# A hybrid decoder layer on one core: cached attention of the decoded rows, two rows on shared partitions

## The chip, the core and the metric

The kernel runs on one core of a Trainium2 chip. The core has a matrix engine (TensorE, PE in the profile), a vector engine (VectorE, DVE), a scalar engine (ScalarE, ACT), a general engine (GpSimd, POOL) and a queue engine (SyncE, SP) that here only issues transfers. Each works through its own list of instructions in order, and semaphores make one wait for another. On-chip memory has 128 partitions; matmuls write to PSUM banks. The metric is the device time of one launch in microseconds: 1455.61 us as the median of 3 runs (1454.94 to 1456.85). About 0.2% of it, 2.9 us, is what these runs can tell from no change.

## The reference

One layer of a decoder is applied to a prompt of 256 tokens and to 8 decoded rows (one new token of each of 8 sequences), with d = 2048 in float32. The two share all weights, so the kernel carries them as N = 264 columns of one matrix. The part that matters here is the attention to memory, 4 heads of width 512 and 256 memory tokens:

```
xq = (rmsnorm(x, g_xa) @ w_xa_q).reshape(B, L, XA_HEADS, XA_DH)
s = jnp.einsum('blhd,bmhd->bhlm', xq, mk.astype(dt)).astype(jnp.float32) * (XA_DH ** -0.5)
p = jax.nn.softmax(s, axis=-1).astype(dt)
o = jnp.einsum('bhlm,bmhd->blhd', p, mv.astype(dt)).reshape(B, L, D_MODEL)
x = x + o @ w_xa_o
```

For the prompt, keys and values mk, mv are computed from a memory of 256 tokens by w_xa_k and w_xa_v. For the decoded rows they come from a cache: every row b and head h has its own 256 x 512 keys and values. So each decoded row is a query vector against matrices of its own, 512 KB of K and 512 KB of V for each of 32 pairs of row and head. Before this part lie a recurrent mixer and its output projection, behind it a feed-forward block with three times 2048 x 5632 weights, and a last norm.

## The kernel before

Everything is held transposed: channels on the partitions in blocks of 128, tokens along the free dimension. A projection goes through a list of steps, `steps`. A step of 2048 x 128 weights loads two halves of 128 x 1024 (SP's queue, tile `raw`, three steps ahead), splits each into a high and a low part in float32r (tile `w`: ACT copies the high part, DVE subtracts to get the low one) and multiplies: 48 matmuls of 264 columns for 16 blocks of channels, three each (high x high, high x low, low x high). `w` has four buffers, each of half a step, so a split waits until PE has read the half-step four earlier, and a step's split is emitted one step ahead of its matmuls with high priority.

The order of the work: the steps run in program order, and beside them stand generators ("side work") that the function `pump` advances after every step, until the planned clocks of DVE and ACT reach that of PE plus 0.5 us. A `yield STEP` ends a generator's turn in that step. The framework's scheduler then orders each engine's list from priorities and dependencies; only SP's list, and PE's in a few places, is kept as written.

The steps around the change are: 16 blocks of `w_q` (the query projection; `evac_q` takes each block's 256 prompt columns into a tile and its 8 decoded columns into `qsm`), then for each head four steps of `w_k` and four of `w_v` for the prompt's memory, then 16 steps of `w_o`. Two generators do the decoded rows' attention beside them, from the fourth block of `w_q` on:

- `dec_k` (line 1167) goes over heads and rows. For each it loads `kc` (128 channels x 4 blocks x 256 tokens) and `vc` from POOL's queue into buffers of the pool `B` (26 buffers), multiplies the four channel blocks of K by the query's per-partition scalars and adds them up in `acc` (first product on ACT, three multiply-adds on DVE), and splits `acc` into `ds` (high on ACT, low on POOL, line 1187).
- `dec_v` (line 1191) sums `ds` over the partitions with two matmuls against `onesr`, a 128 x 128 matrix of ones, which leaves the scores on all partitions (tile `ax`). It takes the maximum (DVE), the exponential and its sum (ACT), and multiplies the four blocks of V by the probabilities with an accumulated sum (DVE), into `osm`. At a head's end `osm` is divided by the sum of the exponentials and `st["dh"]` tells `attend(h)` that the head is done.

`attend(h)` is the prompt's attention; its last part copies and splits `osm` into the columns 256 to 263 of the operands of `w_o` (tiles `oh` and `ol`, groups `B<-osm`). The first `w_o` steps multiply the blocks of heads 0 to 2 first, and those of head 3 when they are there (`pe_o`, line 1361).

The loops and lists are in these functions:

Of the kernel before, what the change touches and what calls it, by code (L numbers as in the profile page):

```python
# [22 lines left out]
N = T + NS  # L23
RGB = 8
H = 4
# [16 lines left out]
STEP = object()  # L42
# [52 lines left out]
def layer_kernel(ctx: ExitStack, tc, xT, memT, vec, wrg, w_in, w_out, w_q, w_k, w_v, w_o,  # L95
# [39 lines left out]
    class Arr:  # L135


        def __init__(self, nb, w=N, dt=F32):
            self.t, self.nb, self.w, self.dt = {}, nb, w, dt
# [7 lines left out]
        def __call__(self, c):  # L147
            return self.tile(c // 4)[:, c % 4, :]
# [119 lines left out]
    def unturn(ps):  # L268

        return ps.rearrange("p (a b) -> p b a", b=2)  # L270
# [9 lines left out]
    st = {}  # L280
# [63 lines left out]
    onesr = const.tile([P, P], F32R, name="onesr")  # L344
# [799 lines left out]
    qsm = const.tile([P, KC, NS], F32, name="qsm")  # L1144
    osm = const.tile([P, KC, NS], F32, name="osm")
    ssm = const.tile([P, H, NS], F32, name="ssm")

    def evac_q(j):
        def f(ps):
            if j == 0:  # L1150
                qn["t"] = Arr(KC, T)
            p2, m = unturn(ps[:, :N]), N // 2
            dve.tensor_mul(qn["t"](j)[:, :m], p2[:, 0, :], rstd[:, :m])
            dve.tensor_mul(qn["t"](j)[:, m:T], p2[:, 1, : T - m], rstd[:, m:T])
            dve.tensor_mul(qsm[:, j, :], p2[:, 1, T - m:], rstd[:, T:N])
            qn["n"] = j + 1
            if j == 3:
                with tc.issue_after(st["split"].ins):
                    act.activation(onesr, ones, AF.Copy)
                st["dk"] = side(dec_k(), 5)  # L1160
                st["dv"] = side(dec_v(), 4)
        return f

    pairs = []
    infl = {"n": 0}

    def dec_k():
        for h in range(H):
            while qn["n"] < 4 * h + 4:
                yield STEP  # L1170
            for b in range(NS):
                while infl["n"] >= NFL:
                    yield STEP
                infl["n"] += 1
                kc = B([P, 4, T])
                pool_e.dma_start(kc, kcT[h, b])  # L1176
                w = sb.tile([P, 264], F32, tag="dw", bufs=2, name=nm("dw"))
                ws = sb.tile([P, 2, T], F32R, tag="ds", bufs=2, name=nm("ds"))
                vc = B([P, 4, T])
                pool_e.dma_start(vc, vcT[h, b])  # L1180
                acc = w[:, 0:T]
                q = [qsm[:, 4 * h + c, b: b + 1] for c in range(4)]
                act.activation(acc, kc[:, 0, :], AF.Copy, scale=q[0])
                for c in range(1, 4):
                    dve.scalar_tensor_tensor(acc, kc[:, c, :], q[c], acc, op0=OP.mult, op1=OP.add)
                act.activation(ws[:, 0], acc, AF.Copy)
                pool_e.tensor_sub(ws[:, 1], acc, ws[:, 0].bitcast(F32))  # L1187
                pairs.append((h, b, w, vc, ws))
                yield 1.1

    def dec_v():
        done, cur = 0, None
        while done < H * NS:
            nxt = None
            if pairs:
                nxt = pairs.pop(0)
                ps = bank("ax")
                pe.matmul(by2(ps[:, :T]), onesr, turn(nxt[4][:, 0]), start=True, stop=False)
                pe.matmul(by2(ps[:, :T]), onesr, turn(nxt[4][:, 1]), start=False, stop=True)
# [5 lines left out]
            h, b, w, vc, _, ps = todo  # L1205
            mx, p = w[:, T: T + 1], w[:, :T]
            dve.tensor_reduce(mx, ps[:, :T], axis=AX.X, op=OP.max)
            dve.tensor_scalar(mx, mx, -XSCALE, None, op0=OP.mult)
            act.activation(halves(p), unturn(ps[:, :T]), AF.Exp, scale=XSCALE, bias=mx,
                           accum_out=ssm[:, h, b: b + 1])  # L1210
            yield 0.5
            for c in range(4):
                dve.scalar_tensor_tensor(vc[:, c, :], vc[:, c, :], 1.0, p, op0=OP.mult, op1=OP.mult,
                                         accum_out=osm[:, 4 * h + c, b: b + 1])
            infl["n"] -= 1
            done += 1
            if done % NS == 0:
# [244 lines left out]
    for i, (src, cols, pef, evf, need) in enumerate(steps):  # L1462
# [26 lines left out]
        ps = pef(i)  # L1489
# [147 lines left out]
```

## Time and profile before

| What | Number |
|---|---|
| median of 3 runs | 1455.61 us |
| the profiled execution | 1455.66 us |
| its span, first to last instruction | 1453.9 us |
| PE busy | 1439.6 us, 99% |
| DVE busy | 1046.8 us, 72% |
| ACT busy | 794.4 us, 55% |
| POOL busy | 129.7 us, 9% |
| read from HBM, written | 314.36 MB, 12.86 MB |

The span begins with the first instruction and leaves out 1.8 us of the execution's own time. Busy time of PE counts overlapping matmuls once, and the mean of one matmul (for example 279 ns) is its time from issue to end, of which the next one overlaps a part; how fast PE really goes is seen from the distance between starts. In the profile's groups, `out<-in` names tiles, and most lines are L60, a helper that records the operations. "Idle before" is time in which the engine stood still just before that group, with the engine that ended it.

### The profile page before, as it was taken

How to read it: one execution, taken by the hardware profiler on the slowest of the kernel's cores; microseconds unless marked ns; L12 is line 12 of the kernel's file. 1: busy time of each engine (PE TensorE's matmuls, PEld its weight loads, DVE VectorE, ACT ScalarE, POOL GpSimd, SP SyncE). 2: the span in 40 equal slices, each digit the busy share in tenths (PEclk: the TensorE clock that was granted, in tenths of full speed). 3: DMA queues.
4: the chain of work that ended last, by engine and by line, in shares of the span. 5: the costliest groups of instructions: out<-in, count | busy, mean ns of one | idle time of the engine just before them, and what ended most of it. 6: DMA issues, size and time to landing. Idle time of an engine off the chain costs nothing.

```text
span 1453.9 us, 30117 instructions
## 1 busy us (share of the span) xinstructions
PE 1439.6 (99%) x12059; PEld 1413.9 (97%) x12059; DVE 1046.8 (72%) x1999; ACT 794.4 (55%) x1279; POOL 129.7 (9%) x206
## 2 busy tenths in 40 slices
PE   9999999999999999999999999999999999999997
PEld 8998999999999999999999999999999999999997
DVE  7966897898899999977676565555656655556564
ACT  7678685665556666656554444334444434444463
POOL 0001210000124343410000000000000000000000
PEclk9999999999999999999999999999999999999999
DMA  9755996558789977955666565655555565656573
GB/s 284 236 174 170 305 378 235 174 169 282 268 328 358 340 288 286 364 175 196 195 192 199 191 200 191 197 195 195 197 196 196 191 201 190 199 192 197 166 239 126
DMA packets 100766, 329.18 MB, mean 226 GB/s; under 512 B 11057, under 2 KB 19937, under 8 KB 100625
## 3 DMA queue, kind: packets, MB, share of 16 engines
q1 hardware_dynamic: 84336, 271.95, 56.2%
q0 software_dynamic: 15424, 54.22, 10.3%
q8 instruction: 94, 1.54, 0.4%
q10 hardware_dynamic: 864, 1.09, 0.2%
q14 instruction: 48, 0.39, 0.1%
HBM read 314.36 MB, written 12.86 MB: 225 GB/s over the span
## 4 chain that ended last, share of the span: by engine, by line
PE 56%; DVE 1%; issue 1%; POOL 0%; ACT 0%; DVEq 0%; DMA 0%; POOLq 0%; ACTq 0%
PE mm L60 55%; PE ax L60 1%; DVE B L60 1%; DVE dw L60 0%; POOL ds L1187 0%; DVE w L60 0%; POOL B L1241 0%; ACT B L60 0%; DVE c L60 0%; POOL o_v L1285 0%; ACT dw L60 0%; DVE t L60 0%; ACT ds L60 0%; DMA o_k<-t 0%; DVEq L1614 0%
## 5 line engine op out<-in xcount | busy, mean ns | idle before, releaser
L60 PE MATMUL mm<-B,w 128*128 128x264 f32 (+1 forms) x10960 | 1281.7, 279 | 2.7 <-DVE w L60 2.3
L60 PEld LDWEIGHTS mm<-B,w 128*128 128x128 f32 x10960 | 1260.8, 189 | 11.1 <-DVE w L60 2.8
L60 DVE TENSOR_TENSOR w<-raw,w 128x1024 fp32r<-128x1024 f32 (+1 forms) x522 | 625.3, 1200 | 307.7 <-ACT w L60 307.1
L60 ACT ACTIVATE w<-raw 128x1024 fp32r<-128x1024 f32 (+1 forms) x522 | 536.3, 1029 | 524.0 <-PE mm L60 358.4
L60 PE MATMUL mm<-w,B 128*128 128x512 f32 x384 | 86.9, 380 | 0.1
L60 PEld LDWEIGHTS mm<-w,B 128*128 128x128 f32 x384 | 70.6, 189 | 9.8 <-DVE w L60 0.5
L1526 POOL TENSOR_TENSOR B<-B,rstd 128x264 f32<-128x264 f32 x4 | 2.8, 740 | 802.9 <-ACT rstd L60 802.9
L60 DVE TENSOR_TENSOR t<-mm,rstd 128x264 f32<-128x264 f32 x96 | 41.5, 433 | 28.9 <-PE mm L60 28.8
L60 DVE SCALAR_TENSOR_TENSOR B<-B,dw 128x256 f32<-128x256 f32 x128 | 53.4, 471 | 3.2 <-ACT dw L60 3.0
L60 DVE TENSOR_TENSOR xres<-xres,mm 128x264 f32<-128x264 f32 (+1 forms) x81 | 34.3, 425 | 29.2 <-PE mm L60 29.2
L60 DVE SCALAR_TENSOR_TENSOR dw<-B,qsm,dw 128x256 f32<-128x256 f32 x96 | 49.1, 516 | 2.5 <-ACT dw L60 1.7
L1187 POOL TENSOR_TENSOR ds<-dw,ds 128x256 fp32r<-128x256 f32 x32 | 36.2, 1131 | 106.5 <-ACT ds L60 106.4
L60 PE MATMUL ax<-B,B 128*128 128x256 f32 (+3 forms) x280 | 44.3, 300 | 0.0
L60 PEld LDWEIGHTS ax<-B,B 128*128 128x128 f32 x280 | 38.8, 191 | 1.9
L60 ACT ACTIVATE B<-xres,vecs 128x264 fp32r<-128x264 f32 (+1 forms) x64 | 32.3, 504 | 3.1 <-DVE xres L60 1.6
L60 ACT ACTIVATE t<-xres 128x264 f32<-128x264 f32 (+1 forms) x53 | 21.1, 410 | 16.2 <-DVE xres L60 16.2
L60 ACT ACTIVATE dw<-B,qsm 128x256 f32<-128x256 f32 x32 | 16.3, 509 | 23.7 <-issue 10.0
L1176 POOL DMA_DIRECT2D B<-kcT x32 | 17.4, 544 | 116.4 <-DVE B L60 103.3
L60 DVE SCALAR_TENSOR_TENSOR B<-xres,vecs,B 128x264 fp32r<-128x264 f32 x48 | 23.4, 489 | 4.0 <-ACT B L60 4.0
L60 ACT ACTIVATE dw<-B,B 128x128 f32<-128x128 f32 x64 | 20.8, 393 | 9.0 <-DMA B<-scr 6.4
L60 ACT ACTIVATE B<-t 128x264 fp32r<-128x264 f32 (+1 forms) x60 | 24.2, 410 | 2.1 <-DVE t L60 2.1
L60 ACT ACTIVATE dw<-ax,dw 128x256 f32<-128x256 f32 x32 | 15.0, 470 | 18.8 <-DVE dw L60 16.7
(173 smaller groups left out, 696.7 us busy)
## 6 DMA issues: line engine op xcount, KB each, us to landing
raw<-w_gu SPq DMA_DIRECT2D x176, 512.0 KB, 4.3
raw<-w_d SPq DMA_DIRECT2D x80, 512.0 KB, 3.6
raw<-w_in SPq DMA_DIRECT2D x74, 512.0 KB, 5.4
raw<-w_out SPq DMA_DIRECT2D x32, 512.0 KB, 4.2
B<-kcT POOLq DMA_DIRECT2D x32, 512.0 KB, 8.7
raw<-w_q SPq DMA_DIRECT2D x32, 512.0 KB, 5.6
B<-vcT POOLq DMA_DIRECT2D x32, 512.0 KB, 10.0
raw<-w_k SPq DMA_DIRECT2D x32, 512.0 KB, 4.9
```

Of the source, the lines that this page charges most:

```text
L60: return f(*a, **k)
L1176: pool_e.dma_start(kc, kcT[h, b])
L1187: pool_e.tensor_sub(ws[:, 1], acc, ws[:, 0].bitcast(F32))
L1526: e.tensor_mul(st["y"](c), st["y"](c), r)
```

## The change

Two decoded rows are put on the 128 partitions together, row 2b on partitions 0 to 63 and row 2b+1 on 64 to 127. A partition then holds 8 blocks of 256 tokens of one row's K (two neighbouring channels' four blocks) where it held 4. So there are 16 pairs instead of 32 rows, and each pair has eight products on K (one on ACT, seven on DVE) and eight on V. `onesr` becomes block-diagonal, ones in the two 64 x 64 corners, so that one pair of matmuls gives both rows' scores, each on its own half of the partitions. Maximum, scaling, exponential, split and subtraction are done once for a pair.

K and V no longer take a new buffer for each row. Each has a `Ring` of two buffers of half a pair, loaded with 128 partitions of 4 KB (`load`, called again when a half has been read). The queries have to be moved to the new partitions (`swap_q`: a POOL copy and four POOL transfers of 64 partitions x 64 bytes for each head) and the outputs back (`swap_o`). The sum over partitions of a pair is taken one step later than before, by one more `yield STEP` ahead of `pairs.append`.

```diff
+            if j % 4 == 3:
+                swap_q(j // 4)
             if j == 3:
                 with tc.issue_after(st["split"].ins):
-                    act.activation(onesr, ones, AF.Copy)
+                    act.activation(onesr, ones, AF.Copy, scale=0.0)
+                    for part in (LOW, HIGH):
+                        act.activation(onesr[part, part], ones[part, part], AF.Copy)
...
+    NB2 = NS // 2
+    q2 = const.tile([P, H, 2, 4, NB2], F32, name="q2")
+    q3 = const.tile([P, 2, 2, 4, NB2], F32, name="q3")
+    o2, o3 = q2, q3
+    LOW, HIGH = slice(0, 64), slice(64, P)
+    by_row = lambda x: x.rearrange("p c (b s) -> p s c b", s=2)
+    def swap_q(h):
+        pool_e.tensor_copy(q3[:, h % 2], by_row(qsm[:, 4 * h: 4 * h + 4, :]))
+        for q, part in enumerate((LOW, HIGH)):
+            for e in range(2):
+                pool_e.dma_start(q2[part, h, e], q3[e: P: 2, h % 2, q])
+    def swap_o(h):
+        rec = ssm[:, h, 0: NB2]
+        dve.reciprocal(rec, rec)
+        o = o2[:, h].rearrange("p g c b -> p (g c) b")
+        dve.tensor_mul(o, o, rec.rearrange("p (c b) -> p c b", c=1).to_broadcast([P, 8, NB2]))
+        for q, part in enumerate((LOW, HIGH)):
+            for e in range(2):
+                pool_e.dma_start(o3[e: P: 2, h % 2, q], o2[part, h, e])
+        pool_e.tensor_copy(by_row(osm[:, 4 * h: 4 * h + 4, :]), o3[:, h % 2])
+    class Ring:
+        def __init__(self, src):
+            self.t, self.at = [B([P, 4, T]), B([P, 4, T])], 0
+            self.src = src.rearrange("h b p c t -> h (b p) c t")
+            self.load()
+            self.load()
+        def load(self):
+            u = self.at
+            if u < H * NB2 * 2:
+                self.at = u + 1
+                b = u // 2 % NB2 * 2 * P + u % 2
+                pool_e.dma_start(self.t[u % 2], self.src[u // NS, b: b + 2 * P - 1: 2])
+        def __call__(self, j):
+            return self.t[j // 4][:, j % 4, :]
     def dec_k():
+        kr = Ring(kcT)
+        st["vr"] = Ring(vcT)
+        yield STEP
...
-                kc = B([P, 4, T])
-                pool_e.dma_start(kc, kcT[h, b])
...
-                vc = B([P, 4, T])
-                pool_e.dma_start(vc, vcT[h, b])
                 acc = w[:, 0:T]
-                q = [qsm[:, 4 * h + c, b: b + 1] for c in range(4)]
-                act.activation(acc, kc[:, 0, :], AF.Copy, scale=q[0])
-                for c in range(1, 4):
-                    dve.scalar_tensor_tensor(acc, kc[:, c, :], q[c], acc, op0=OP.mult, op1=OP.add)
+                for j in range(8):
+                    q = q2[:, h, j // 4, j % 4, b: b + 1]
+                    if j == 0:
+                        act.activation(acc, kr(0), AF.Copy, scale=q)
+                    else:
+                        dve.scalar_tensor_tensor(acc, kr(j), q, acc, op0=OP.mult, op1=OP.add)
+                    if j % 4 == 3:
+                        kr.load()
+                    if j == 3:
+                        yield 1.0
                 act.activation(ws[:, 0], acc, AF.Copy)
                 pool_e.tensor_sub(ws[:, 1], acc, ws[:, 0].bitcast(F32))
-                pairs.append((h, b, w, vc, ws))
                 yield 1.1
+                yield STEP
+                pairs.append((h, b, w, ws))
...
-            for c in range(4):
-                dve.scalar_tensor_tensor(vc[:, c, :], vc[:, c, :], 1.0, p, op0=OP.mult, op1=OP.mult,
-                                         accum_out=osm[:, 4 * h + c, b: b + 1])
+            for j in range(8):
+                v = st["vr"](j)
+                dve.scalar_tensor_tensor(v, v, 1.0, p, op0=OP.mult, op1=OP.mult,
+                                         accum_out=o2[:, h, j // 4, j % 4, b: b + 1])
+                if j % 4 == 3:
+                    st["vr"].load()
+                if j == 3:
+                    yield 1.0
...
-            if done % NS == 0:
-                dve.reciprocal(ssm[:, h, :], ssm[:, h, :])
-                for c in range(4):
-                    dve.tensor_mul(osm[:, 4 * h + c, :], osm[:, 4 * h + c, :], ssm[:, h, :])
+            if done % NB2 == 0:
+                swap_o(h)
+                yield STEP
                 st["dh"] = h + 1
```

The lists of the engines change at three places that the prediction speaks of. A row has the line, the operation, the tiles written and read, and the size; `x3` stands for three alike in a row.

DVE in the query projection, before: `dw_5218` is the first row's sum of products on K, `dw_5230` the second row's, each K tile (`B_5216`, `B_5228`) with a buffer of its own; `w` rows are the weight splits of the running steps.

```order
L60 TENSOR_TENSOR w_5097<-raw_5027,w_5097 128x8x128
L60 SCALAR_TENSOR_TENSOR dw_5218<-B_5216,qsm,dw_5218 128x256 x2
L60 TENSOR_TENSOR w_5157<-raw_5087,w_5157 128x8x128
L60 TENSOR_TENSOR B_4966<-mm_5100,rstd 128x132
L60 TENSOR_TENSOR B_4966<-mm_5100,rstd 128x124
L60 TENSOR_TENSOR qsm<-mm_5100,rstd 128x8
L60 SCALAR_TENSOR_TENSOR dw_5218<-B_5216,qsm,dw_5218 128x256
L60 TENSOR_TENSOR w_5160<-raw_5089,w_5160 128x8x128
L60 SCALAR_TENSOR_TENSOR dw_5230<-B_5228,qsm,dw_5230 128x256 x3
```

DVE there now, two steps later: `dw_5296` is the first pair, `dw_5372` the second, `B_5225` and `B_5226` are K's ring, and `q_117` the moved queries (`q2`).

```order
L60 SCALAR_TENSOR_TENSOR dw_5296<-B_5225,q_117,dw_5296 128x256 x3
L60 TENSOR_TENSOR w_5313<-raw_5221,w_5313 128x8x128
L60 SCALAR_TENSOR_TENSOR dw_5296<-B_5226,q_117,dw_5296 128x256
L60 TENSOR_TENSOR B_5233<-mm_5243,rstd 128x132
L60 TENSOR_TENSOR B_5233<-mm_5243,rstd 128x124
L60 TENSOR_TENSOR qsm<-mm_5243,rstd 128x8
L60 SCALAR_TENSOR_TENSOR dw_5296<-B_5226,q_117,dw_5296 128x256 x2
L60 TENSOR_TENSOR w_5316<-raw_5223,w_5316 128x8x128
L60 SCALAR_TENSOR_TENSOR dw_5296<-B_5226,q_117,dw_5296 128x256
L60 SCALAR_TENSOR_TENSOR dw_5372<-B_5225,q_117,dw_5372 128x256 x2
L60 TENSOR_TENSOR w_5389<-raw_5292,w_5389 128x8x128
```

Between the last read of `B_5225` for the first pair and its first read for the second stand two weight splits, in which the ring's buffer has to be loaded again.

POOL's list at the same time, before: loads of K and V (`kcT`, `vcT`) and the subtraction for the split of `ds`.

```order
L1176 DMA B_5216<-kcT 128x1024
L1180 DMA B_5220<-vcT 128x1024
L1176 DMA B_5228<-kcT 128x1024
L1180 DMA B_5232<-vcT 128x1024
L1187 TENSOR_TENSOR ds_5219<-dw_5218,ds_5219 128x256
L1187 TENSOR_TENSOR ds_5231<-dw_5230,ds_5231 128x256
L1176 DMA B_5378<-kcT 128x1024
L1180 DMA B_5382<-vcT 128x1024
```

POOL's list there now; `q_118` is `q3`, the copy from which the transfers into `q2` read, `B_5229` and `B_5230` are V's ring.

```order
L1206 DMA B_5225<-kcT 128x1024
L1206 DMA B_5226<-kcT 128x1024
L1206 DMA B_5229<-vcT 128x1024
L1206 DMA B_5230<-vcT 128x1024
L1179 COPY q_118<-qsm 128x32
L1182 DMA q_117<-q_118 64x16 x4
L1206 DMA B_5225<-kcT 128x1024
L1206 DMA B_5226<-kcT 128x1024
L1236 TENSOR_TENSOR ds_5297<-dw_5296,ds_5297 128x256
```

The loads are the same in number and size, but the next ones of K stand behind the exchange and wait for the reads of the same buffers.

PE at the third and fourth step of `w_o`, before: `mm_1100_8532` is the third step's output, `w_1091_8446` its second half of weights, `mm_1106_8597` the fourth step's, and `ax_1087_8428` the last part of the prompt's attention of head 3.

```order
L60 MATMUL ax_1087_8428<-B_1081_8390,B_1074_8331 128x256 x2
L60 MATMUL ax_1087_8428<-B_1081_8390,B_1075_8332 128x256
L60 MATMUL mm_1100_8532<-B_1033_7997,w_1091_8446 128x264
L60 MATMUL mm_1100_8532<-B_1034_7998,w_1091_8446 128x264
L60 MATMUL mm_1100_8532<-B_1033_7997,w_1091_8446 128x264 x2
L60 MATMUL mm_1100_8532<-B_1034_7998,w_1091_8446 128x264
L60 MATMUL mm_1100_8532<-B_1033_7997,w_1091_8446 128x264
L60 MATMUL mm_1106_8597<-B_853_6844,w_1098_8526 128x264
L60 MATMUL mm_1106_8597<-B_854_6845,w_1098_8526 128x264
L60 MATMUL mm_1079_8348<-B_1083_8400,w_1071_8293 128x264
L60 MATMUL mm_1092_8449<-B_1083_8400,w_1078_8345 128x264
```

PE there now: `mm_992_8344` is the third step, with its first half of weights (`w_982_8255`) ending in the first row and its second half (`w_983_8258`) behind, and `mm_998_8409` is the fourth.

```order
L60 MATMUL mm_992_8344<-B_851_7210,w_982_8255 128x264
L60 MATMUL mm_992_8344<-B_918_7729,w_983_8258 128x264
L60 MATMUL mm_992_8344<-B_919_7730,w_983_8258 128x264
L60 MATMUL mm_992_8344<-B_918_7729,w_983_8258 128x264 x2
L60 MATMUL mm_992_8344<-B_919_7730,w_983_8258 128x264
L60 MATMUL mm_992_8344<-B_918_7729,w_983_8258 128x264 x2
L60 MATMUL mm_992_8344<-B_919_7730,w_983_8258 128x264
L60 MATMUL mm_992_8344<-B_918_7729,w_983_8258 128x264 x2
L60 MATMUL mm_992_8344<-B_919_7730,w_983_8258 128x264
L60 MATMUL mm_992_8344<-B_918_7729,w_983_8258 128x264
L60 MATMUL mm_998_8409<-B_783_6674,w_990_8338 128x264
L60 MATMUL mm_998_8409<-B_784_6675,w_990_8338 128x264
```

Head 3's blocks of the first three steps stand behind these rows in both orders, so two of the four `w` buffers are held until then. The attention's last part (24 matmuls) stood among the third step's second half before; now it has moved up to the beginning of the second step, and only the 12 matmuls of `w_983_8258` stand between the end of `w_982_8255` and the fourth step.

More of the change, by code (lines that the diff above doesn't have):

```diff
@@ L1170, in dec_k @@
                 yield STEP
-            for b in range(NS):
+            for b in range(NB2):
                 while infl["n"] >= NFL:
@@ L1174, in dec_k @@
                 infl["n"] += 1
-                kc = B([P, 4, T])
-                pool_e.dma_start(kc, kcT[h, b])
                 w = sb.tile([P, 264], F32, tag="dw", bufs=2, name=nm("dw"))
                 ws = sb.tile([P, 2, T], F32R, tag="ds", bufs=2, name=nm("ds"))
-                vc = B([P, 4, T])
-                pool_e.dma_start(vc, vcT[h, b])
                 acc = w[:, 0:T]
-                q = [qsm[:, 4 * h + c, b: b + 1] for c in range(4)]
-                act.activation(acc, kc[:, 0, :], AF.Copy, scale=q[0])
-                for c in range(1, 4):
-                    dve.scalar_tensor_tensor(acc, kc[:, c, :], q[c], acc, op0=OP.mult, op1=OP.add)
+                for j in range(8):
[8 more added lines that the diff above has]
+                        yield 1.0
                 act.activation(ws[:, 0], acc, AF.Copy)
                 pool_e.tensor_sub(ws[:, 1], acc, ws[:, 0].bitcast(F32))
-                pairs.append((h, b, w, vc, ws))
                 yield 1.1
+                yield STEP
+                pairs.append((h, b, w, ws))
     def dec_v():
         done, cur = 0, None
-        while done < H * NS:
+        while done < H * NB2:
             nxt = None
@@ L1197, in dec_v @@
                 ps = bank("ax")
-                pe.matmul(by2(ps[:, :T]), onesr, turn(nxt[4][:, 0]), start=True, stop=False)
-                pe.matmul(by2(ps[:, :T]), onesr, turn(nxt[4][:, 1]), start=False, stop=True)
+                pe.matmul(by2(ps[:, :T]), onesr, turn(nxt[3][:, 0]), start=True, stop=False)
+                pe.matmul(by2(ps[:, :T]), onesr, turn(nxt[3][:, 1]), start=False, stop=True)
                 nxt += (ps,)
@@ L1204, in dec_v @@
                 continue
-            h, b, w, vc, _, ps = todo
+            h, b, w, _, ps = todo
             mx, p = w[:, T: T + 1], w[:, :T]
```

## The prediction

> **What bounds the kernel now.** I read the page first, then the work of each engine by stage, then what TensorE waited for in the stage that the change touches.
>
> ```profile
> span 1453.9 us, 30117 instructions
> ...
> PE 1439.6 (99%) x12059; PEld 1413.9 (97%) x12059; DVE 1046.8 (72%) x1999; ACT 794.4 (55%) x1279; POOL 129.7 (9%) x206
> ```
>
> TensorE (PE) works through 99% of the span. So what counts is how much PE work goes away, and whether PE has to wait anywhere new. The decoded rows' attention lies between 320 and 660 us. In the table by stretch the columns are PE, its weight loads (PEld), VectorE (DVE), ScalarE (ACT), GpSimd (POOL), the granted clock, the DMA engines' share and GB/s:
>
> ```profile
> 320.00:460.00 140.00, 139.88 (x1198) 138.27 (x1197) 126.51 (x295) 79.85 (x125) 29.20 (x46) 1.00 0.82 292
> 460.00:560.00 100.00, 100.00 (x584) 91.07 (x583) 97.79 (x237) 64.68 (x126) 41.51 (x54) 1.00 0.90 334
> 560.00:660.00 100.00, 99.68 (x647) 91.85 (x647) 87.93 (x225) 63.31 (x133) 28.36 (x38) 1.00 0.69 246
> ```
>
> The granted clock is 1.00 throughout. PE has no holes, while DVE is close behind it: 97.79 of 100 us in the middle. A stall of DVE is the danger; ACT and POOL have room. These are all the waits of PE and of its weight loads from 320 to 660 us (total, times, longest):
>
> ```profile
> PE ax L60 <- POOL ds L1187: 0.2, 1, 0.2
> ...
> PEld ax L60 <- POOL ds L1187: 1.3, 3, 0.7
> PEld mm L60 <- DVE w L60: 0.5, 1, 0.5
> PEld ax L60 <- ACT ds L60: 0.2, 1, 0.2
> ```
>
> Nearly all of it is the decode's own sums over partitions (ax from ds) waiting for POOL.
>
> **The change, part by part.** The groups of this stage that it touches, and the weight splits beside them (busy us, mean ns of one | idle before):
>
> ```profile
> L60 DVE TENSOR_TENSOR w<-raw,w 128x1024 fp32r<-128x1024 f32 x118 | 149.1, 1268 | 15.5 <-ACT w L60 15.2
> ...
> L60 ACT ACTIVATE w<-raw 128x1024 fp32r<-128x1024 f32 x116 | 122.0, 1054 | 56.8 <-PE mm L60 39.5 <-issue 6.4 <-ACT t L60 4.5
> ...
> L60 DVE SCALAR_TENSOR_TENSOR B<-B,dw 128x256 f32<-128x256 f32 x128 | 53.4, 471 | 3.2 <-ACT dw L60 3.0
> L60 DVE SCALAR_TENSOR_TENSOR dw<-B,qsm,dw 128x256 f32<-128x256 f32 x96 | 49.1, 516 | 2.5 <-ACT dw L60 1.7
> L1187 POOL TENSOR_TENSOR ds<-dw,ds 128x256 fp32r<-128x256 f32 x32 | 36.2, 1131 | 106.5 <-ACT ds L60 106.4
> ...
> L60 PE MATMUL ax<-ds,onesr 128*128 128x256 f32 x64 | 17.4, 283 | 0.4 <-POOL ds L1187 0.2
> L1176 POOL DMA_DIRECT2D B<-kcT x32 | 17.4, 544 | 116.4 <-DVE B L60 103.3 <-ACT w L60 4.0 <-ACT ds L60 3.7
> ...
> L60 ACT ACTIVATE dw<-B,qsm 128x256 f32<-128x256 f32 x32 | 16.3, 509 | 23.7 <-issue 10.0 <-DVE B L60 5.3 <-DMA B<-kcT 4.3
> L1241 POOL TENSOR_TENSOR B<-t,B 128x256 fp32r<-128x256 f32 x16 | 15.8, 998 | 2.1 <-ACT B L60 1.9
> L60 ACT ACTIVATE dw<-ax,dw 128x256 f32<-128x256 f32 x32 | 15.0, 470 | 18.8 <-DVE dw L60 16.7 <-PE mm L60 1.2 <-POOL ds L1187 0.8
> L60 ACT ACTIVATE ds<-dw 128x256 fp32r<-128x256 f32 x32 | 13.3, 415 | 20.2 <-DVE dw L60 20.2
> L60 DVE TENSOR_REDUCE dw<-ax 128x1 f32<-128x256 f32 x32 | 13.2, 416 | 0.0
> ...
> L60 DVE TENSOR_TENSOR B<-mm,B 128x512 fp32r<-128x512 f32 x8 | 5.1, 684 | 0.0
> ...
> L60 DVE TENSOR_SCALAR dw<-dw 128x1 f32<-128x1 f32 x32 | 4.7, 148 | 0.2
> ...
> L60 ACT ACTIVATE B<-osm 128x8 fp32r<-128x8 f32 x16 | 2.0, 198 | 0.0
> ...
> L60 DVE TENSOR_TENSOR B<-osm,B 128x8 fp32r<-128x8 f32 x16 | 1.6, 159 | 0.0
> L60 DVE TENSOR_TENSOR osm<-osm,ssm 128x8 f32<-128x8 f32 x16 | 1.6, 158 | 0.0
> ```
>
> *PE.* Two rows share the 128 partitions, so 16 pairs replace 32 rows: 64 sum matmuls become 32. Their price is not the mean of 283 ns, since matmuls overlap. PE's timeline has the pitch:
>
> ```profile
> 387.62 0.38 PE L60 MATMUL ax<-ds,onesr 128*128 128x256 f32 x2
> 387.84 5.57 PE L60 MATMUL mm<-B,w 128*128 128x264 f32 x48
> 393.25 0.38 PE L60 MATMUL ax<-ds,onesr 128*128 128x256 f32 x2
> ```
>
> Two sums take from 387.62 to 387.84, so 0.11 us each; a step of 48 matmuls takes 5.41 us, 0.113 each. The bounds are 32 x 0.11 = 3.5 us and, by busy time, 17.4/2 = 8.7 us. I take 3.5: on a full PE, the pitch is what frees time. This lies wholly on the path.
>
> *Sums one step later.* The sum of a pair is emitted one more step behind its multiply-adds, which gives POOL's subtraction 5.4 us more. The 1.7 us of waits on ds (0.2 + 1.3 + 0.2) can go; at worst all stay. Half as many sums alone suggest 0.8 us gained, which I take.
>
> *DVE.* A pair has 7 multiply-adds on K where two rows had 6: +16 x 0.516 = +8.3 us. Maximum and scaling halve: -16 x (0.416 + 0.148) = -9.0. Scaling the outputs is one wide operation per head instead of four, -12 x 0.158 = -1.9 us. Net about -2.7 us. The 128 products with V stay.
>
> *ACT.* 16 each of first product, copy and exponential go: -16 x (0.509 + 0.415 + 0.470) = -22.3 us. The two more copies into onesr are under a microsecond, far ahead of use. Off the path, but ACT's half of the splits gets nearer to hand.
>
> *POOL.* 16 subtractions go: -16 x 1.131 = -18.1 us. The exchange between rows and partitions adds 8 copies and 32 small DMA issues, 32 x 0.544 = 17.4 us. No row shows such a copy: nothing to 1.13 us each, I take 0.3 as it has 32 columns against 256. Sum about 0, not on the path. The first exchange has to land before the first product: 0.3 + 4 x 0.54 and a landing of up to 3.7 us (a row below) make 6.2, and the new order puts the product three half-steps (8.1 us) behind the fourth query block, so it is covered; the decode starts two steps later and is not on PE's path until w_o. On the way back POOL's copy stands until its four DMAs have landed, with subtractions and K and V issues queued behind: 2 to 4 us, three times in the middle, where the next K halves have three to eight splits of time.
>
> POOL's subtraction also costs DVE time. DVE rows, then POOL's, of the same moment:
>
> ```profile
> 411.43 0.42 DVE L60 SCALAR_TENSOR_TENSOR B<-B,dw 128x256 f32<-128x256 f32 x1
> 411.78 0.08 DVE L60 DVE_READ_ACCUMULATOR B<-B,dw 128x1 f32 x1
> 411.78 1.16 DVE L60 SCALAR_TENSOR_TENSOR B<-B,dw 128x256 f32<-128x256 f32 x1
> ...
> 411.91 0.74 POOL L1187 TENSOR_TENSOR ds<-dw,ds 128x256 fp32r<-128x256 f32 x1
> ```
>
> One product took 0.42 us alone and 1.16 beside POOL. Over the stage the products with V are (0.471 - 0.42) x 128 = 6.5 us over that; shared by POOL's 48 subtractions (32 here, 16 on L1241), 0.14 us each, so 16 fewer give DVE 2 us. The Trainium skill (SBUF — State Buffer, Who interferes with whom) has DVE with two SBUF inputs blocked for the whole of a GpSimd instruction that reads SBUF; by it 16 x 0.74 = 11.8 us would come free. The row agrees with the rule, the mean with a part of it. Either way it makes DVE's cover thicker and takes nothing off PE.
>
> *Loads.* Before, each row takes fresh buffers of a pool of 26 and loads run far ahead. After, K and V each have a ring of two half-pairs, and half u+2 is only issued when half u has been read. The bytes are the same. What covers this is the splits' lead: w has four half-step buffers, so a split may start three half-steps ahead of its use, 3 x 2.7 = 8.1 us, and takes 1.05 + 1.27 = 2.3; 5.8 us of lead. Time from a K issue to landing, in 330 to 360 and in 375 to 390 us:
>
> ```profile
> DMA to landing us min/median/max: 4.5/6.3/8.0
> ...
> DMA to landing us min/median/max: 7.0/9.5/13.6
> ```
>
> In the changed order most halves have three to nine splits between freeing and next use, 8 to 24 us. Seven have only two, 5.4 us (both K halves of the second pair, one each of the sixth, eighth and tenth, both V halves of the last). At 6.3 to 9.5 us they come 0.9 to 4.1 late, inside the 5.8. The second row is six loads issued at once, which rings of two no longer do. I take no PE stall, and keep 2.4 us (13.6 - 5.4 - 5.8) per half as the upper end. The Trainium skill (DMA: Bandwidth & Descriptors, Anatomy of one DMA) fits 2.0 us plus bytes at 436 GB/s, an estimate of 3.2 us for 512 KB, by which no half would be late. The rows with weights streaming beside are two to three times that, so they decide.
>
> *The end.* The last head's outputs now pass four DMAs and a POOL copy before ACT and DVE split them. Small POOL transfers landed in
>
> ```profile
> o_h<-hlast POOLq DMA_DIRECT2D x1, 36.0 KB, 3.7
> ...
> o_sn<-snew POOLq DMA_DIRECT2D x1, 16.0 KB, 1.7
> ```
>
> New there: 4 x 0.54 + 1.7 to 3.7 + 0.3 = 4.2 to 6.2 us. PE's cover: between the last sums and the first use of these outputs the new order has 134 matmuls and 4 transposes, 138 x 0.113 = 15.5 us. Against that stand, from the last V step's end, on DVE: the rest of the pair before 0.4, two weight splits 2.5, a maximum 0.4, three 512-wide subtractions 1.9 (5.2); eight products at 0.417 less their overlap 2.8, a split and three short operations 1.9; the exchange 4.2; ACT's four copies 0.8 and DVE's four 0.6: 15.5. It just meets, and is 2.0 late with the slow landing. Besides, two of the four w buffers are held there by the delayed matmuls, so the split for the fourth w_o step starts only when the third step's first half has been read, 12 matmuls (1.35 us) ahead of its use, and takes 2.3: PE waits 1.0. Before, 24 matmuls of the prompt's attention stood there too, 2.7 us more. I take 1.0, with bounds 0 and 3.0.
>
> **Sum.** The profiled execution took 1455.66 us, 1.8 more than its span; the median is 1455.61, so it stands for the runs. -3.5 - 0.8 + 1.0 = -3.3 us: 1452.4.
>
> **Rivals.** *Late halves (slower).* A K or V half arrives after the lead is used up; ACT or DVE stand at it in order, with weight splits queued behind, and PE waits for w. For it: DVE has 2% free in the middle, so lateness adds up. Against it: ACT waited for K loads before only 4.3 us in all, and no PE wait came of it. It decides from 11.2 us of landing (5.4 + 5.8). Four of the seven at 2.4 us: 1452.4 + 9.6 = 1462.0. By the Trainium skill (SBUF — State Buffer, two separate sides) a DMA issued by POOL cannot get its descriptors written while DVE holds their shared port; that would lengthen landings, and no row here separates it.
>
> *Gain given back at the joints.* The exchange at the end lands slowly or the fourth split comes later, and a short wait at the first pairs: 2 to 5 us, 1454 to 1457, inside 0.2% of now. For it: my sum there has nothing to spare. Against: the waits it replaces also lay there.
>
> *More than the pitch.* All 1.7 us of ds waits vanish and the end fits: 1455.66 - 5.2 = 1450.5.
>
> *The change doesn't do what it says.* The order has 32 sums and one step more; only the time could stay, if the pitch were not what frees PE: 1455.7.
>
> **How the numbers follow.** 0.2% is 2.9 us, about what a measurement of this kernel tells from no change. My forecast with the larger gain, under 1452.7: 0.48. Given back, or no effect: 0.32. Late halves: 0.20. The range goes from 1450.3, all waits gone, to 1460, part of the late halves; the forecast's own is 1450.3 to 1454.
>
> **What would show it.** Right: the sum group at x32, PE's waits in the stage still under 3 us, DVE's split idle unchanged, landings under 11 us. Wrong: PE waiting for DVE w or ACT w, ACT dw waiting for kcT by tens of us, or a hole in PE just before the first outputs' projection (w_o).

## The result and the profile after

The changed kernel took 1461.21 us (median of 10 runs, 1457.91 to 1462.67) against 1455.46 us for the kernel before in the same comparison (10 runs). The ratio is 1.0036, 95% interval 1.0028 to 1.0043: slower by 0.36%, where 0.2% less time was forecast. The profiled execution took 1460.49 us, its span 4.9 us more than before's. Ratios in this document are of undisturbed runs: one of the 11 runs of the kernel with three buffers in each ring took 2526.76 us at a granted clock of 0.555 and is not in its ratio.

The head of its page, and the two busiest of the three stretches of the decoded rows' attention (columns as before: PE, PEld, DVE, ACT, POOL, clock, DMA share, GB/s):

```profile
span 1458.8 us, 29940 instructions
...
PE 1437.9 (99%) x12027; PEld 1410.7 (97%) x12027; DVE 1042.8 (71%) x1971; ACT 770.5 (53%) x1217; POOL 127.3 (9%) x230
```

```profile
320.00:460.00 140.00, 138.43 (x1188) 136.91 (x1187) 120.58 (x270) 70.75 (x101) 31.30 (x55) 1.00 0.80 270
460.00:560.00 100.00, 95.94 (x550) 85.90 (x550) 94.44 (x224) 55.21 (x104) 34.40 (x55) 1.00 0.89 310
```

The work shrank as planned: every engine is less busy. But PE, which had no holes, now stands still for 1.6 and 4.1 us in these two stretches, and DVE did 6 us less work by 460 us (120.58 against 126.51). That DVE is less busy is here a bad sign: it waits (with three buffers for K, below, it works 125.56 us in the same stretch). The waits from 320 to 660 us say for what:

```profile
ACT dw L60 <- DMA B<-kcT: 22.7, 5, 5.7
...
DVE dw L60 <- DMA B<-kcT: 6.6, 4, 3.4
...
PEld mm L60 <- DVE w L60: 5.0, 5, 1.9
...
PE mm L60 <- DVE w L60: 3.5, 4, 1.6
...
PE ax L60 <- ACT ds L60: 1.2, 1, 1.2
...
PE ax L60 <- DVE B L60: 1.0, 1, 1.0
...
PE ax L60 <- ACT B L60: 0.4, 1, 0.4
```

ACT and DVE wait 29.3 us for halves of K (4.3 us before), and PE waits for split weights (DVE w), for which it had not waited at all; only a weight load had, 0.5 us. The groups that answer to those of before:

```profile
L60 DVE SCALAR_TENSOR_TENSOR dw<-B,q,dw 128x256 f32<-128x256 f32 x112 | 58.0, 520 | 9.0 <-DMA B<-kcT 6.6 <-ACT dw L60 1.4
L60 DVE SCALAR_TENSOR_TENSOR B<-B,dw 128x256 f32<-128x256 f32 x128 | 48.5, 441 | 1.9 <-ACT dw L60 1.1 <-DMA B<-vcT 0.6
...
L60 ACT ACTIVATE dw<-B,q 128x256 f32<-128x256 f32 x16 | 8.1, 509 | 39.6 <-DMA B<-kcT 22.7 <-issue 10.7 <-DVE B L60 4.4
...
L60 PE MATMUL ax<-ds,onesr 128*128 128x256 f32 x32 | 6.6, 283 | 1.2 <-ACT ds L60 1.2
```

How a wait for K becomes a hole of PE is seen in four engines' timelines of one place. First DVE, then POOL, ACT, DVE again and PE:

```profile
422.51 1.22 DVE L60 TENSOR_TENSOR w<-raw,w 128x1024 fp32r<-128x1024 f32 x1
427.08 0.48 DVE L60 SCALAR_TENSOR_TENSOR dw<-B,q,dw 128x256 f32<-128x256 f32 x1 [3.35 <-DMA B<-kcT]
...
440.44 1.01 DVE L60 SCALAR_TENSOR_TENSOR dw<-B,q,dw 128x256 f32<-128x256 f32 x2
```

```profile
441.47 0.53 POOL L1206 DMA_DIRECT2D B<-kcT  x1 [4.11 <-DMA B<-vcT]
```

```profile
441.03 1.05 ACT L60 ACTIVATE w<-raw 128x1024 fp32r<-128x1024 f32 x1
447.59 0.51 ACT L60 ACTIVATE dw<-B,q 128x256 f32<-128x256 f32 x1 [5.51 <-DMA B<-kcT]
448.01 1.99 ACT L60 ACTIVATE w<-raw 128x1024 fp32r<-128x1024 f32 x2
```

```profile
444.60 0.42 DVE L60 SCALAR_TENSOR_TENSOR B<-B,dw 128x256 f32<-128x256 f32 x1 [0.64 <-DMA B<-vcT]
...
446.92 1.21 DVE L60 TENSOR_TENSOR w<-raw,w 128x1024 fp32r<-128x1024 f32 x1
```

```profile
435.75 10.88 PE L60 MATMUL mm<-B,w 128*128 128x264 f32 x87
448.19 7.95 PE L60 MATMUL mm<-B,w 128*128 128x256 f32 x47 [1.57 <-DVE w L60]
```

DVE stood 3.35 us at a K half, with a weight split queued behind it. From 427.1 to 448.1 its timeline shows no gap but one of 0.64 us, so it never made the delay up; the split that PE needed at 446.6 ended at 448.1, and PE stood 1.57 us. ACT's wait of 5.51 us shows the ring: the buffer was read by 440.9, asked for at 441.47 (POOL's bracket names a load of V, but the issue came 0.55 us after that read), filled by 447.5, and ACT wanted it at 442.1.

The lead of the splits can be worked out from the two traces: the time from the end of a DVE split to the start of the first matmul that waits for it, splits and half-steps matched in order. From 380 to 400 us its median is 5.8 us in both kernels. In the next three stretches of 20 us it is 5.5, 4.4 and 3.8 us before, and 3.6, 2.0 and 1.1 after.

### The profile page after: what moved, and what is told of

Same layout as the page of the kernel before. It is cut to its first block, busy times and chain, and to the rows that moved or that the text cites. A ratio compares the mean times of both kernels' runs of the same rounds, so it can differ in the third digit from the quotient of the medians.

```text
span 1458.8 us, 29940 instructions
## 1 busy us (share of the span) xinstructions
PE 1437.9 (99%) x12027; PEld 1410.7 (97%) x12027; DVE 1042.8 (71%) x1971; ACT 770.5 (53%) x1217; POOL 127.3 (9%) x230
## 4 chain that ended last, share of the span: by engine, by line
PE 65%; DVE 1%; issue 1%; DMA 0%; ACT 0%; POOL 0%; DVEq 0%; POOLq 0%
PE mm L60 63%; PE ax L60 2%; DVE B L60 1%; DVE w L60 0%; DMA o_v<-B 0%; DVE dw L60 0%; ACT w L60 0%; DVE c L60 0%; DVE t L60 0%; POOL ds L1236 0%; POOL B L1206 0%; POOL o_v L1339 0%; DVEq L1668 0%; ACT t L60 0%; ACT c L60 0%
## 5 line engine op out<-in xcount | busy, mean ns | idle before, releaser
L60 DVE SCALAR_TENSOR_TENSOR dw<-B,q,dw 128x256 f32<-128x256 f32 x112 | 58.0, 520 | 9.0 <-DMA B<-kcT 6.6
L60 DVE SCALAR_TENSOR_TENSOR B<-B,dw 128x256 f32<-128x256 f32 x128 | 48.5, 441 | 1.9 <-ACT dw L60 1.1
L60 ACT ACTIVATE dw<-B,q 128x256 f32<-128x256 f32 x16 | 8.1, 509 | 39.6 <-DMA B<-kcT 22.7
L60 PE MATMUL ax<-B,w 128*128 128x264 f32 x144 | 22.7, 286 | 1.7 <-ACT w L60 1.7
L60 PEld LDWEIGHTS ax<-B,w 128*128 128x128 f32 x144 | 19.9, 194 | 2.6 <-ACT w L60 2.5
```

The source lines that it names most:

```text
L60: return f(*a, **k)
```

## The experiments

PE is the clock of this kernel, so each profiled run can be booked by PE alone. A hole here is the distance from one matmul's start to the next, less the median distance for its width (0.113 us at 264 columns, 0.216 at 512, 0.110 at 256), summed over the trace. But for its two ends, the span is the sum of all these distances, so the first two columns add up to it by construction: the book sorts a change of time, it does not prove a price. Differences to the kernel before (holes 18.1 us in all, 1.6 of them from 320 to 720 us), in us:

| kernel | sums left out x 0.11 | holes | sum of both | span measured |
|---|---|---|---|---|
| changed | -3.5 | +8.3 | +4.8 | +4.9 |
| three buffers, K and V | -3.5 | -0.6 | -4.2 | -4.2 |
| three buffers, K alone | -3.5 | -0.3 | -3.8 | -3.9 |
| three buffers, V alone | -3.5 | +7.0 | +3.5 | +3.4 |
| changed, without the step | -3.5 | +16.1 | +12.6 | +12.6 |
| before, half the sums | -3.5 | +4.6 | +1.1 | +1.0 |
| before, rings of two | 0 | +6.4 | +6.4 | +6.5 |

What the traces do show is that the three distances are the same in every kernel, so all that needs an explanation is holes. (Of the changed kernel's 8.3 us, 7.2 lie between 320 and 720 us, and 1.2 us at 150 to 200 us, in a stage the change does not touch, where the holes are 3.0 to 4.6 us in all the kernels.)

Three theories stood against each other. A: K's ring of two halves refills too late. B: the added step itself makes the engines bunch. C: POOL's queue, now with the exchange in it, issues the loads late.

**Three half buffers in each ring.**

```diff
-            self.t, self.at = [B([P, 4, T]), B([P, 4, T])], 0
+            self.t, self.at, self.used, self.n = [B([P, 4, T]) for _ in range(n)], 0, -n, n
...
-        kr = Ring(kcT)
-        st["vr"] = Ring(vcT)
+        kr = Ring(kcT, 3)
+        st["vr"] = Ring(vcT, 3)
```

> The changed kernel with three half buffers in each ring instead of two, so that a half is asked for a whole half earlier. The orders of ACT, DVE and PE stay as they are but for a few rows. Theory A (late halves: the ring refills too late, ACT and DVE stand at K with weight splits queued behind): the waits of ACT and DVE for kcT fall from 29 us (22.7 + 6.6) to under 4, the holes of PE between 440 and 515 us from about 7 us to under 2, the time to 1452 to 1455 us, that is 0.1 to 0.25% under the kernel before. Theory B (the sums and so the whole chain stand one block later, and this makes DVE and ACT bunch): waits for kcT go, the holes stay, 1459 to 1461. Theory C (POOL's queue, with the exchange in it, issues the loads late): a third buffer helps in part, 1457 to 1459.

Measured: 1453.37 us, ratio to before 0.9989 (0.9980 to 0.9998). The waits for K fell from 29.3 to 2.7 us, PE's for w to 1.0. A is borne out; B and C had put the time at 1457 or more.

**Three buffers for K alone, and for V alone.** The same edit with 3 and 2, and 2 and 3.

> The changed kernel with a third half buffer for K alone; V keeps two. The order of PE is that of the changed kernel row for row, ACT's and DVE's differ in 10 and 41 lines of a comparison. Theory A (K late): nearly the whole of what three buffers on both rings gave, 1453 to 1455 us, waits for kcT under 4 us, PE's holes between 440 and 515 us under 2. If V's lateness or the shifted order gave the gain: 1457 to 1461.

> The changed kernel with a third half buffer for V alone. Theory A: no gain, 1459 to 1462 us, ACT's waits for kcT still over 15 us. If any freer queue of POOL or any small shift of the order gives the gain: 1453 to 1456.

K alone: 1452.86 us, 0.9984 (0.9975 to 0.9993). V alone: 1460.39, 1.0040 (1.0026 to 1.0054). PE's order is the changed kernel's row for row in the first, so its gain is not one of order on PE (a few rows of DVE, ACT and POOL moved). The two stretches with K's third buffer, and its waits for K from 320 to 660 us:

```profile
320.00:460.00 140.00, 140.00 (x1193) 138.44 (x1192) 125.56 (x286) 74.75 (x107) 35.17 (x61) 1.00 0.84 294
460.00:560.00 100.00, 99.88 (x584) 90.71 (x583) 96.47 (x226) 59.12 (x110) 34.12 (x56) 1.00 0.91 320
```

```profile
PEld mm L60 <- DVE w L60: 1.4, 2, 0.8
...
DVE dw L60 <- DMA B<-kcT: 1.4, 1, 1.4
PEld mm L60 <- ACT B L60: 1.3, 1, 1.3
...
PE mm L60 <- ACT B L60: 1.1, 1, 1.1
...
PE mm L60 <- DVE w L60: 0.7, 1, 0.7
```

With V's third buffer alone the waits stay:

```profile
ACT dw L60 <- DMA B<-kcT: 25.3, 5, 5.7
...
DVE dw L60 <- DMA B<-kcT: 4.1, 4, 1.8
...
PE mm L60 <- DVE w L60: 3.8, 7, 1.1
```

PE is full again in the stage (140.00 of 140.00) where K has three. Worked out from POOL's issues and the first reads: with two buffers, 10 of 30 K halves are read less than 9 us after their issue (the earliest after 4.9), with three 1 of 29, and the median goes from 11.6 to 17.6 us. The landings (6.8 and 7.1 us, medians of the two pages) did not get shorter; the ask came earlier.

**The added step taken out.**

```diff
                 yield 1.1
-                yield STEP
                 pairs.append((h, b, w, ws))
```

> The changed kernel without the one added step between a pair's multiply-adds and its sums. Theory A: next to no change, 1459 to 1462 us, with ACT's waits for kcT still over 15 us. Theory B: the holes of PE between 440 and 515 us go, 1453 to 1456. By the prediction's step on the sums one block later, the waits of PE for ds come back, 1 to 2 us more.

Measured: 1470.42 us, 1.0105 (1.0092 to 1.0119): 9 us slower than the changed kernel, more than any of the three theories gave. B is out, but A's "next to no change" was wrong too. With three buffers:

> Three half buffers on both rings and the added step between multiply-adds and sums taken out: the step's worth without K's lateness. The step without three buffers was worth 9 us. If it is worth that by its own (PE stands at the sums for ds, which ACT and POOL have not written yet): 1461 to 1465 us, waits of PE and its loads for ds over 12 us, waits for kcT under 4. If it only hid K's lateness: 1452 to 1456. By the prediction's 0.8 us for the step: 1454 to 1455.

Measured: 1461.14 us, 1.0045 (1.0033 to 1.0058), 7.8 us more than with the step. Its waits from 320 to 660 us:

```profile
DVE dw L60 <- DMA B<-kcT: 10.9, 3, 6.4
...
PEld ax L60 <- ACT ds L60: 9.1, 4, 7.0
PE ax L60 <- ACT ds L60: 8.0, 3, 6.7
...
ACT dw L60 <- DMA B<-kcT: 2.4, 1, 2.4
...
PEld ax L60 <- POOL ds L1236: 1.5, 2, 1.2
```

PE stands at the sums for ds, 9.0 us in all and once for 6.7 us; with the step and three buffers PE itself waits for no ds. The expected end of the waits for K did not come here (13.3 us). The order of all engines is another one without the step; what of it makes K late again is not shown.

**The step alone, in the kernel before.**

```diff
-                pairs.append((h, b, w, vc, ws))
                 yield 1.1
+                yield STEP
+                pairs.append((h, b, w, vc, ws))
```

> The kernel before with the added step alone: each row's sums go out one block later, rows not shared, loads as before. If the step frees PE of waits for ds: 1453.5 to 1455 us (there were only 1.7 us of them). If the step by itself makes DVE and ACT bunch: 1457 to 1462. The rows in flight stay at two, so a row takes longer, and the decode's end comes later: a hole before w_o is the third way, 1456 to 1460.

Measured: 1474.85 us, 1.0137 (1.0123 to 1.0150). It was the third way, and much dearer than I put it. PE's timeline at the end of the decode:

```profile
656.72 1.41 PE L60 MATMUL ax<-ds,onesr 128*128 128x256 f32 x4
664.23 0.58 PE L60 MATMUL ax<-ds,onesr 128*128 128x256 f32 x1 [6.10 <-ACT ds L60]
...
672.53 17.67 PE L60 MATMUL mm<-B,w 128*128 128x264 f32 x128 [3.12 <-ACT B L60]
```

Only two rows may be in flight, so a step more for each of 32 rows made the decode end late: the last sums stand at 664 to 668 us, and w_o waits for them. Holes from 640 to 680 us come to 20.5 us; ahead of that, from 320 to 640 us, to 0.3 (the waits for ds there are gone). ACT waited 15.6 us for K in that stretch, in nine waits of up to 3.1 us, and PE had no hole from them: the sum of such waits alone does not say what PE loses. With 16 pairs the same step costs half as many blocks, and the decode ends in time.

**The price of a sum.** The kernel before with one sum per row, the second of the two left out:

```diff
-                pe.matmul(by2(ps[:, :T]), onesr, turn(nxt[4][:, 0]), start=True, stop=False)
-                pe.matmul(by2(ps[:, :T]), onesr, turn(nxt[4][:, 1]), start=False, stop=True)
+                pe.matmul(by2(ps[:, :T]), onesr, turn(nxt[4][:, 0]), start=True, stop=True)
```

> The kernel before with the second of the two sum matmuls of each row left out (32 of 64; the low half of the products' sum is then missing from the scores). It measures the disputed price alone. At the pitch of 0.11 us: 3.5 us less, 1452 us, ratio 0.9976. If the waits for ds that came with them go as well: 1450.5. If sums lie in holes of PE: 1455.5, no change.

Measured: 1455.98 us, 1.0009 (1.0000 to 1.0018). Taken by its time alone, the sums would be worth nothing. The waits show what took the gain:

```profile
PEld ax L60 <- ACT ds L60: 5.7, 7, 2.0
...
PE ax L60 <- ACT ds L60: 3.2, 5, 1.6
```

With fewer matmuls the scheduler placed the remaining sums elsewhere (line by line, PE's rows in the two traces differ in 438 lines, where 32 sums went), where ds was not ready. In the book above that is -3.5 for the sums and +4.6 for new holes.

**Rings of two in the kernel before.**

```diff
-                kc = B([P, 4, T])
-                pool_e.dma_start(kc, kcT[h, b])
+                kc = kr()
...
+                kr.load()
                 act.activation(ws[:, 0], acc, AF.Copy)
```

> The kernel before, one row after the other, but with K and V each in a ring of two buffers, the next row's load issued when its buffer has been read, as in the changed kernel; nothing else is changed. Theory A: the ring alone makes the kernel slower, by 3 to 8 us, 1458.5 to 1463.5, with tens of us of ACT and DVE waits for kcT and vcT and PE waiting for DVE w. Theories B and C: within 0.15% of before, 1453.5 to 1457.5.

Measured: 1462.09 us, 1.0048 (1.0036 to 1.0061). The time is what A expected, the reason is not: there is no wait for kcT or vcT in the stage at all. PE's own waits are these:

```profile
PEld ax L60 <- POOL ds L1203: 4.8, 5, 1.5
...
PEld ax L60 <- ACT ds L60: 3.7, 4, 1.3
...
PE ax L60 <- POOL ds L1203: 3.3, 5, 1.2
PE ax L60 <- ACT ds L60: 2.4, 3, 1.0
```

Two buffers that each hold a whole row are a full row of lead, where two halves of a pair are only one pair in all; so this run was no test of the changed ring. In four of PE's five waits for POOL, the issue of a K load (0.53 us) stands directly ahead of the subtraction that PE waits for, and PE's order moved as well (422 lines). How much of the 6.4 us of holes each of these costs is open.

**Shorter loads of K.** After the first two, each K load fetches one chunk of four; the scores are then computed from stale rows.

```diff
-                pool_e.dma_start(self.t[u % 2], self.src[u // NS, b: b + 2 * P - 1: 2])
+                c = slice(0, 1 if self.short and u > 1 else 4)
+                pool_e.dma_start(self.t[u % 2][:, c], self.src[u // NS, b: b + 2 * P - 1: 2][:, c])
```

> The changed kernel, rings of two, but every load of a K half after the first two fetches only the first of its four chunks (a quarter of the bytes; the other chunks keep stale rows, so the scores are not those of the reference). The ring is as shallow, only the landing is shorter. Theory A (a half's use comes 5 to 9 us after its issue, its landing takes 5 to 8): K lands in 2.5 to 4 us, the waits for kcT fall under 8 us, PE's holes between 440 and 515 us under 3, the time 1452 to 1456 us. If what matters is the instant of issue or the queue and not the landing: 1458 to 1462.

Measured: 1454.90 us, 1.0001 (0.9993 to 1.0010); waits for K 3.3 us. But it does not tell landing from issue. A quarter of the bytes took nearly as long to land (median 5.8 us from 395 to 640 us, 2.6 to 9.9), and since only chunk 0 is written, the load could be issued as soon as the first product had read it, mostly 2 to 10 us ahead of the half's last read. The run agrees with A; that the landing was what mattered is not shown.

**The exchange on SP's queue.**

```diff
-                pool_e.dma_start(q2[part, h, e], q3[e: P: 2, h % 2, q])
+                sp.dma_start(q2[part, h, e], q3[e: P: 2, h % 2, q])
...
-                pool_e.dma_start(o3[e: P: 2, h % 2, q], o2[part, h, e])
+                sp.dma_start(o3[e: P: 2, h % 2, q], o2[part, h, e])
```

> The changed kernel with the exchange's 32 small DMAs issued by SP instead of POOL, so that no K or V load stands behind them. Theory A: no gain, 1459 to 1463 us, or a little more where a weight load stands behind one of them on SP. Theory C (the exchange on POOL's queue issues the loads late): 1453 to 1456. In the trace of the changed kernel four K halves of 30 were issued more than 1 us after their buffer was free, 2.8 at most, which is why little is expected.

Measured: 1462.30 us, 1.0048 (1.0036 to 1.0060): no gain. It is not a clean answer. Waits for K fell to 5.5 us, but SP now stood at the exchange (12.1 us once ahead of 640 us), and weights came late behind it (ACT's and PE's waits, 400 to 520 us):

```profile
ACT w L60 <- DMA raw<-w_q: 6.4, 3, 3.2
...
ACT w L60 <- DMA raw<-w_k: 4.0, 3, 1.6
PE mm L60 <- DVE w L60: 3.9, 5, 1.5
```

What it does show is that late issues are not the cause: all 30 halves were now issued within 0.7 us of being free, and still 10 of them were read less than 9 us after their issue, as in the changed kernel. There, 26 of the 30 were issued within 1 us of being free, and the halves that ACT or DVE waited longest for (5.7, 5.51, 4.80, 3.87 and 3.35 us) within 0.6. Three that were issued 2.0, 2.2 and 2.8 us late made DVE wait 1.46, 1.19 and 0.58 us, 3.2 of the 29.3. So C explains little of the lateness.

**The end, with three buffers for K.** Holes of 2.2 us stood from 640 to 680 us, where w_o needs the last head's outputs (0.6 with three buffers in both rings). Two edits at that place, the step left out for the last two pairs, and two of the last four transfers on SP:

```diff
-                yield STEP
+                if h * NB2 + b < H * NB2 - 2:
+                    yield STEP
```

```diff
-                pool_e.dma_start(o3[e: P: 2, h % 2, q], o2[part, h, e])
+                (sp if e and h == H - 1 else pool_e).dma_start(o3[e: P: 2, h % 2, q], o2[part, h, e])
```

> Three half buffers for K, two for V, and the added step left out for the last two of the 16 pairs, so that the decode ends a block earlier. With three buffers for K, 2.3 us of PE's holes stood at the first w_o outputs (640 to 660 us), behind the last exchange. If the sums of the last pairs find ds written: 1450.5 to 1452 us. If PE stands at them for ds, as it did without the step: 1453 to 1456.

> Three half buffers for K, two for V, and in the last head's exchange of outputs two of the four DMAs issued by SP instead of POOL, beside the other two. POOL spent 2.1 us on issuing the four, one after the other, and 1.45 more until the last had landed; two and two should end about 1 us sooner. PE waited 1.1 us for the outputs there: 1451.5 to 1453 us, 0.5 to 1 us under the kernel with three K buffers. If a weight load comes late behind them on SP, or the wait for w (0.7 us) is what ends last: 1452.5 to 1454.

Measured: 1453.39 us, 0.9990 (0.9982 to 0.9999), and 1452.06 us, 0.9979 (0.9970 to 0.9987). Both close the hole. From 640 to 680 us, K's third buffer alone, then the second edit:

```profile
640.00:680.00 40.00, 38.27 (x337) 37.88 (x336) 29.07 (x54) 20.23 (x33) 3.05 (x5) 1.00 0.58 192
```

```profile
640.00:680.00 40.00, 40.00 (x358) 40.00 (x357) 29.27 (x62) 22.36 (x38) 2.34 (x5) 1.00 0.65 228
```

In both, holes of about the same sum opened earlier in the stage, as the edits moved rows there. The last kernel has the lowest median of all measured, under both kernels of this case; from K's third buffer alone (0.9984) it can't be told apart.

## Why the prediction was wrong

The step that failed is *Loads*: "I take no PE stall". It rests on two figures, 5.4 us from a half's freeing to its next use and 5.8 us of lead, and neither held where it was needed. The parts of it, and the other steps:

- **Which halves.** The prediction named five K halves and two of V. Waits came for nine K halves: the first of the second pair, and both of the fourth, sixth, eighth and tenth, where one each of the sixth, eighth and tenth were named. The last pair's V halves, named too, were not waited for; one other half of V cost 0.6 us.
- **The 5.4 us from freeing to use.** This is two splits at PE's pace of 2.7 us. Worked out from POOL's issues and the starts less the waits, DVE came to the halves that it waited for 5.1 to 5.9 us after their issue, as counted. But ACT, which reads a pair's first chunk, came to its five 0.6 to 3.1 us after their issue. Those five are 22.7 of the 29.3 us.
- **The lead of 5.8 us.** The size was right, where the decode starts: 5.8 us in both traces from 380 to 400 us. The error was to give it to every half anew. Even before the change it shrank to 3.8 us by 440 to 460, since DVE worked 58.35 of 60 us there and had next to no time to build it up again. With the waits of 2.8 and 3.9 us on ACT, and of 1.4 (behind ACT) and 3.35 on DVE, it was down to about 1 us when PE's holes began at 446 us. So K halves that each came late by less than 5.8 us cost 5.7 us of PE's busy time from 320 to 680 us (359.56 to 353.90), and gave 7.2 us more of holes from 320 to 720.
- **Late halves, the rival.** Its mechanism and its place in DVE's full middle were right, and for this I gave it 0.20. That its 1462.0 came so near to 1461.2 is luck: it stands for four halves at 2.4 us each, and nine halves were waited for, 0.6 to 5.7 us. Its deciding point, a landing over 11.2 us, was wrong: from 395 to 640 us no K load took over 8.3 us. Landings became shorter (6.8 against 8.7 us in the page), as I took from the row of six loads issued at once. That spoke for the forecast only because I compared it with the two figures above.
- **The Trainium skill's 3.2 us** (DMA: Bandwidth & Descriptors, Anatomy of one DMA) for 512 KB was half of what the runs show for K beside streaming weights (6.8 us in the page after), as the prediction's rows had it.
- **PE's sums.** -3.5 us at the pitch: the distance of 0.110 us is the same in every trace. The run that was to measure the price alone gave nothing by its time, so no run shows the gain by itself; with K in time the whole change came to -1.6 and -2.1 us against the kernel before in the same comparison.
- **The step.** Put at -0.8 us, the waits of the kernel before. Against the changed kernel without it, it is worth 9.2 us (7.8 with K in time), with the new order of all engines in that price. I priced it by the waits that stood in the order before, not by those of the new order; since the step is part of the change, the sum was not hurt by it.
- **The end.** +1.0 with bounds of 0 and 3: 0.7 us of holes after, and 2.2 with a third buffer for K alone (0.6 with a third one for V too). With K's third buffer the exchange took 4.5 us from its first issue to the end of POOL's copy; 4.2 to 6.2 was the working.
- **DVE, ACT, POOL.** -2.7 and -2 for DVE: 1046.8 to 1042.8. -22.3 for ACT: 794.4 to 770.5. About 0 for POOL: 129.7 to 127.3. Right as busy time, and the saving itself lay off the path.
- **POOL's hold on DVE.** The products with V went from 471 to 441 ns, 3.8 us in all, or 0.24 us for each of 16 subtractions, if they are the whole of it; 2 us was forecast. The rule of the Trainium skill (SBUF — State Buffer, Who interferes with whom) would have given 11.8.

With the ring of two made three for K alone, 1452.86 us stands beside a forecast of 1452.4. In part this is luck: against the kernel before in the same comparison (1455.00) it is -2.1 us where -3.3 was forecast, and the end's holes came to 2.2 us where 1.0 was.

## What to carry to other kernels

When buffers become a ring, write down for each refill when it is free, when it is read, and how long a load takes to land at that moment; take the reading engine's own arrival and not PE's pace; count the lead of the engines behind it once for all refills in a row, not once for each, if the engine that would make it up is busy 97% of the time. A cut of work on the bounding engine is worth its pitch, but an order that a scheduler makes anew can spend more than that in holes (4.6 us against 3.5 here), so book work and holes apart before you call a saving worthless.

## What the runs showed that was not expected

The time to land grows far less than the size while weights stream. These are the transfers of the changed kernel from 395 to 515 us (KB each, median us to landing), at a DMA share of 0.88 to 0.92:

```profile
raw<-w_k SPq DMA_DIRECT2D x16, 512.0 KB, 5.0
B<-kcT POOLq DMA_DIRECT2D x15, 512.0 KB, 6.9
...
o_k<-t POOLq DMA_DIRECT2D x5, 128.0 KB, 6.3
...
q<-q POOLq DMA_DIRECT2D x16, 4.0 KB, 4.6
```

4 KB take two thirds of the time of 512 KB. And leaving 32 matmuls out of a kernel that is bound by matmuls did not make it faster (+1.1 us, within what these runs can tell from no change), since the order moved with them and new holes took the gain.
